# Moving a rarely taken branch and a residual addition inside a stream of expert products

## The chip, the core and the metric

The kernel runs on one core of a Trainium2 chip. That core has a matrix engine (TensorE, PE in the profile, with its weight loads as PEld), a vector engine (VectorE, DVE), a scalar engine (ScalarE, ACT), a general engine (GpSimd, POOL) and a queue engine (SyncE, SP) that here only starts transfers. Each engine runs its own list of instructions in order and waits for the others by semaphores. The metric is the device time of one execution in microseconds.

## The reference

Two layers of a decoder trunk on 256 tokens of width 1024. Each layer has a mixer (three groups of heads behind one projection, and an output projection), a layer norm, a mixture of experts, and a second layer norm. What the change touches is the mixture of experts and the addition before the second norm:

```python
for e in range(N_EXPERTS):                       # 16 experts, hidden width 512
    act = jax.nn.silu(t @ w_gate[e]) * (t @ w_up[e])
    out = out + combine[:, e:e + 1] * (act @ w_down[e])
...
h = layer_norm(DN_ALPHA * h + mix, ln_mix_g[layer], ln_mix_b[layer])
ffn = moe_ffn(h, router_w, router_bias, ...)     # top 2 of 16, within one group of 4
h = layer_norm(DN_ALPHA * h + ffn, ln_ffn_g[layer], ln_ffn_b[layer])
```

Each token goes to two experts; `combine` holds its two weights and zeros. All arithmetic is in float32.

## The kernel before

**Stages.** The mixer of a layer is put in order by a small planner (class `Order`, lines 75 to 236: it estimates when each engine comes free). The mixture of experts behind it (lines 1459 to 1622) is in the order in which its code is written, and the change lies there alone. That order is the same for both layers.

**Experts in pairs.** The loop of line 1538 runs over eight pairs of experts, `p` from 0 to 7. Instead of all 256 tokens, each expert works on 32 slots for each of the two tiles of 128 tokens (`CAP`, line 27): 128 rows for a pair. For each pair there are:
- a gather: one-hot matrices `G` (made on DVE) pick the tokens of two pairs at a time by products on PE, and ACT and DVE write them out scaled, as `xT` (`gather_two`, line 1326; after the up products of pairs 1, 3 and 5, `TWO`, line 59);
- 16 gate products, `gu`, then ACT's silu (line 1544), then 16 up products, in eight steps `k` of two (`step`, line 1514), then DVE's product of the two into `act` (line 1554);
- the pair's slot weights `Gw` (DVE, line 1351), turned on PE into a slot table `sT` and reduced by DVE (`by_slot`, line 1360);
- four transposes of `act` on PE, written out by ACT as `actT` (`turn`, line 1558);
- 16 down products `y` (line 1597), the loop index `i` of line 1593 counting eight steps of two;
- the weighting of their result by ACT and DVE into `yt` (`by_tile`, line 1379), and one pair later the scatter: four products `sc` of `yt` with the slot table, added to the sum `z` by DVE (`scatter`, line 1393).

**Weights.** Every expert matrix passes once through SBUF in tiles of 512 KB. SP issues them in the order of use; 33 buffers (`NFEED`) hold them, and a tile's transfer waits until the tile that had its buffer has been used (`used`, line 330, `more`, line 341). Some tiles are loaded ahead into other buffers (`EXTRA`).

**The overflow branch.** An expert can get more than 32 tokens of a tile. For that case `overflow()` (line 1407) holds a full calculation of all 16 experts on all tokens, with weights for the tokens left over, behind `tc.If(rmax > CAP)`: a compare-and-branch on every engine, on a count read into registers at the end of pair 0 (line 1622). With the inputs of this case it isn't taken. But PE's and DVE's programs hold its instructions, so both jump over them, and on the way past, each engine raises its own semaphore by what the instructions left out would have added. Six of the eight PSUM banks are handed out to it; whoever uses one of these banks next waits until the engines are past the branch. Where it stands is `OVER_AT`: behind up step 5 of pair 5.

**The residual.** `residual(t, n)` (line 1258) adds `alpha * (h * gain + bias)` to half `n` of tile `t` of the sum: three DVE operations `r`, `r`, `z` on 128 x 512. Gain and bias are vectors of the first norm, loaded by GpSimd and broadcast over the partitions (`lnvec`, line 372), in buffers that the down weights of pair 4 leave (`VECS`). `REST` names the four places: up steps 1 and 3 of pair 5 and up steps 1 and 5 of pair 6, as (pair, step).

Of the kernel before, what the change touches and what calls it, by code (L numbers as in the profile page):

```python
# [61 lines left out]
LEAN = 5  # L62
FILL_0 = (2, 3)
SC_AT = 5
OVER_AT = (5, 'u', 5)
REST = ((5, 1), (5, 3), (6, 1), (6, 5))
LAST_AT = 5
PARTED = (2, 3, 4, 5)
VECS = ((4, 2), (4, 3), (4, 5), (5, 3))
# [170 lines left out]
def trunk_kernel(ctx, tc, x, positions, w_in, gate_up, gate_bias, norm_gain, w_out, ln_mix_g, ln_mix_b,  # L240
# [18 lines left out]
    def t2(name, shape=(P, 512), dt=F32):  # L259
        return wp.tile(list(shape), dt, name=name, tag="t2", bufs=N_T2)  # L260
# [4 lines left out]
    def t1(name, shape, dt=F32):  # L265
        return wp.tile(list(shape), dt, name=name, tag="t1", bufs=N_T1)
# [63 lines left out]
    def used(l, p, nm, i, u):  # L330

        if type(u) is not list:
            more()
        elif (p, nm, i) in AGAIN:
            while specs[issued[0]][0] in extra:
                issued[0] += 1
            key, ((_, src),) = specs[issued[0]][0], specs[issued[0]][1][0]
            issued[0] += 1
            feed[key] = apart(place_of[p, nm, i], src)
# [150 lines left out]
    def mm(o, a, b, start=True, stop=True):  # L490
        pe.matmul(o, a, b, start=start, stop=stop, skip_group_check=True)
# [252 lines left out]
    for l in range(DEPTH):  # L744
# [513 lines left out]
        def residual(t, n):  # L1258

            c = slice(512 * n, 512 * n + 512)  # L1260
            r = t2("r")
            dve.scalar_tensor_tensor(r, h[t][:, c], ALPHA, vecs[0][:, c], op0=OP.mult, op1=OP.mult)
            dve.scalar_tensor_tensor(r, vecs[1][:, c], ALPHA, r, op0=OP.mult, op1=OP.add)
            dve.tensor_add(z[t][:, c], z[t][:, c], r)
# [86 lines left out]
        def weights(p):  # L1351

            Gw = t1("Gw", (P, NT, 2, NT * CAP))
            for t in range(NT):
                for e in range(2):
                    c = t * E + 2 * p + e
                    dve.tensor_scalar(Gw[:, t, e], iota, pos[:, c:c + 1], comb[:, c:c + 1], op0=OP.is_equal, op1=OP.mult)
            return Gw
# [20 lines left out]
        def by_tile(ps, ys, ws):  # L1379

            for y in ys:
                act.activation(y, ps, AF.Copy, scale=ws)
            for q in range(P // CAP):
                t = q % NT
                r = slice(q * CAP, (q + 1) * CAP)
                o = slice((q + 1 - 2 * t) * CAP, (q + 2 - 2 * t) * CAP)
                dve.scalar_tensor_tensor(ys[t][o], ps[r], ws[r], ys[t].bitcast(F32)[r], op0=OP.mult, op1=OP.subtract)
# [5 lines left out]
        def scatter(p, yt, sT, tiles=range(NT)):  # L1393
            if p == 0:
                z.extend(t4("z", (P, D)) for _ in range(NT))
            for t in tiles:
                for n in range(2):
                    b_ = bank("sc")
                    mm(b_, sT[:, t * P:(t + 1) * P], yt[n][t])
                    zs = z[t][:, 512 * n:512 * n + 512]  # L1400
                    if p == 0:
                        act.activation(zs, b_, AF.Copy)
                    else:
                        dve.tensor_add(zs, zs, b_)
                    od.free(b_)
# [87 lines left out]
        def part(u, j):  # L1493
            return u[j] if type(u) is list else u[:, j]
# [3 lines left out]
        def part_z(t, n):  # L1498

            if not zs:  # L1500
                zs["I"] = t1("identr", (P, P), F32R)
                act.activation(zs["I"], ident, AF.Copy)
            zs[t, n] = [t2("zs", dt=F32R) for _ in range(2)]
            split(z[t][:, 512 * n:512 * n + 512], *zs[t, n])
# [9 lines left out]
        def step(p, nm, b_, k):  # L1514
            if k % 2 == 0:
                us[nm] = [feed.pop((l, nm, p, k + e)) for e in range(2)]
            for e in range(2):
                mm(b_[64 * e:64 * e + 64], xs[p](k, e), part(us[nm][e], k % 2), start=k == 0, stop=k == KT - 1)
                if k % 2:
                    used(l, p, nm, k - 1 + e, us[nm][e])  # L1520
            if (p, nm) == (FIN, "u") and k in PARTED:
                part_z(*divmod(PARTED.index(k), 2))
            if (p, nm, k) == (FIN, "g", SC_AT):
                scatter(*late.pop())
            if (p, nm, k) == OVER_AT:
                overflow()
            if nm == "u" and (p, k) in REST:
                residual(*divmod(REST.index((p, k)), 2))

        def gate(p, upto):  # L1530

            if p not in gates:
                gates[p], done_k[p] = bank("gu"), 0
            while done_k[p] < upto:
                step(p, "g", gates[p], done_k[p])
                done_k[p] += 1

        for p in range(E // 2):
            final = p == FIN
            if final:  # L1540
                Gw = weights(p)
            gate(p, KT)
            av = t2("act")
            act.activation(av, gates[p], AF.Silu)
            if not final:
                Gw = weights(p)
            if p in TWO:
                G = t1("G", (P, NT, 4, CAP))
                for t in range(NT):
                    slots(G[:, t], t, 2 * p + 2)  # L1550
            bu = bank("gu")
            for k in range(KT):
                step(p, "u", bu, k)
            dve.tensor_mul(av, av, bu)
            od.free(gates[p], bu)
            sT, ws = by_slot(Gw, final)

            def turn():
                b_ = bank("aT")
                b3 = b_.rearrange("p (a n) -> p a n", a=4)  # L1560
                for f in range(4):
                    tr(b3[:, f], av[:, f * P:(f + 1) * P])
                aT = t2("actT", (P, 4, P))
                act.activation(aT, b3, AF.Copy)
                od.free(b_)
                made.append(aT)

            made = []
            if final:
                for n in range(2):  # L1570
                    for t in range(NT):
                        begin(t, n)
                turn()
            elif p == 0:
                gate(1, FILL_0[0])
                turn()
                gate(1, FILL_0[1])
            elif p in TWO:
                gather_two(p + 1, turn, G)
                scatter(*late.pop())  # L1580
            else:
                scatter(*late[0], (0,))
                if p < LEAN:
                    gate(p + 1, FILL[0])
                turn()
                scatter(*late.pop(), (1,))
                if p < LEAN:
                    gate(p + 1, FILL[1])
            aT, = made
            py = [bank("y") for _ in range(2)]  # L1590
            yt = [None, None]
            ud = [feed.pop((l, "d", p, i)) for i in range(8)]
            for i in range(8):
                n, k = (i // 4, i % 4) if p >= FIN - 1 else (i % 2, i // 2)
                for e in range(2):
                    u = ud[2 * k + e]
                    mm(py[n][64 * e:64 * e + 64], aT[:, k, 64 * e:64 * e + 64], part(u, n), start=k == 0, stop=k == 3)
                    if n:
                        if (p, 2 * k + e) in VECS:
                            vecs.append(lnvec((ln_mix_g, ln_mix_b, ln_ffn_g, ln_ffn_b)[len(vecs)], l))  # L1600
                        else:
                            used(l, p, "d", 2 * k + e, u)
                if k == 3:
                    yt[n] = [t2("yt", dt=F32R) for _ in range(2)]
                    if final:
                        split(py[n], *yt[n], scale=ws)
                    else:
                        by_tile(py[n], yt[n], ws)
                if final:
                    t = i - LAST_AT  # L1610
                    if t in range(NT):
                        place(sb[t, 0], t, 0, yt, sT, start=False)
                        sts.append(sm("st", 12).rearrange("p (a b) -> p a b", a=2))
                        dve.bn_stats(sts[t][:, 0], sb[t, 0])
            od.free(*py)
            late.append((p, yt, sT))
            if p == FIN - 1:
                more(2)
                if l + 1 < DEPTH:
                    mixer_constants(l + 1)  # L1620
            if p == 0:
                rmax = nc.values_load(cnti[0:1, 0:1], min_val=0, max_val=L)
# [68 lines left out]
```

## Time and profile before

| what | value |
|---|---|
| median of 3 runs | 736.85 us (736.49 to 737.7) |
| the profiled execution | 737.43 us, span 735.7 us |
| mean granted clock of PE | 0.987 |
| PE busy | 696.5 us, 95% |
| DVE busy | 441.1 us, 60% |
| ACT busy | 269.3 us, 37% |
| read from HBM | 241.08 MB, 329 GB/s over the span |

The span runs from the first to the last instruction in the profile. Times in the rows below are counted from its start. The expert stage of the first layer lies at about 160 to 355 us, that of the second at about 515 to 720 us. A share of busy time is a mean over stages with different limits; where PE waits is told by the list of waits and the timeline. The name behind an arrow in brackets is what ended the wait; `DVEq` and `PEq` are the sequencers of these engines, the parts that take branches and semaphores.

### The profile page before, as it was taken

The page shows a single profiled execution, that of the slowest core. Times are in us where ns is not written, and L with a number is a line of the kernel's source. Part 1 is how long each engine was busy: PE and PEld are TensorE (multiplying, and loading weights), DVE is VectorE, ACT ScalarE, POOL GpSimd, SP SyncE. Part 2 cuts the span into 40 slices and gives each one's busy share as a digit, 9 for nine tenths or more (in the row PEclk, how much of TensorE's full clock was granted, in tenths as well). Part 3 has the DMA queues.
Part 4 walks back from the last instruction along what each step waited for, and adds up shares of the span by engine and source line. Part 5 has one row for each costly group of instructions (what it writes and reads, how often), then busy time and mean ns, then how long its engine had stood idle before and what let it go on. Part 6 is the DMA issues. An engine that isn't in the chain of part 4 may idle for free. (4 is left out here: it accounts for less than half of the span.)

```text
span 735.7 us, 11107 instructions
## 1 busy us (share of the span) xinstructions
PE 696.5 (95%) x3817; PEld 403.2 (55%) x3817; DVE 441.1 (60%) x1115; ACT 269.3 (37%) x549; POOL 44.5 (6%) x72
## 2 busy tenths in 40 slices
PE   7999999999999997999899999999999999959993
PEld 6897977853533432533488788787334343334331
DVE  4897865652454546675498688566244263636645
ACT  5668645431211201212376766564113111102111
POOL 2000001000000001010130000001000000110002
PEclk9999999999999999999999999999999999989997
DMA  8899846879999999999999554667899999999921
GB/s 302 292 393 408 313 150 200 311 265 411 409 402 407 409 408 408 406 408 401 351 387 393 195 172 127 235 195 303 337 406 406 405 407 410 408 406 406 408 91 57
DMA packets 83245, 243.01 MB, mean 330 GB/s; under 512 B 10148, under 2 KB 14312, under 8 KB 83176
## 3 DMA queue, kind: packets, MB, share of 16 engines
q1 hardware_dynamic: 82504, 241.86, 86.5%
q8 instruction: 34, 0.56, 0.3%
q10 hardware_dynamic: 416, 0.26, 0.1%
q14 instruction: 35, 0.29, 0.1%
q0 software_dynamic: 256, 0.03, 0.0%
HBM read 241.08 MB, written 1.05 MB: 329 GB/s over the span
## 5 line engine op out<-in xcount | busy, mean ns | idle before, releaser
L235 PE MATMUL gu<-wf,xT 128*64 128x512 f32 x912 | 226.0, 594 | 3.8 <-PEq L1412 3.8
L235 DVE SCALAR_TENSOR_TENSOR yt<-y,ws,yt 32x512 fp32r<-32x512 f32 (+1 forms) x116 | 86.7, 747 | 103.3 <-ACT yt L235 101.8
L235 PEld LDWEIGHTS gu<-wf,xT 128*64 128x64 f32 x912 | 71.4, 137 | 132.3 <-issue 124.9
L235 DVE TENSOR_TENSOR wlo<-wf,whi 128x512 fp32r<-128x512 f32 (+2 forms) x174 | 97.3, 599 | 38.8 <-ACT whi L235 36.4
L235 PE MATMUL y<-wf,actT 128*64 128x512 f32 x432 | 110.5, 595 | 1.8 <-ACT actT L235 1.8
L235 ACT ACTIVATE whi<-wf 128x512 fp32r<-128x512 f32 (+2 forms) x176 | 86.8, 552 | 13.9 <-PE po L235 9.5
L235 PE MATMUL pj<-whi,hhi 128*128 128x512 f32 (+2 forms) x224 | 81.6, 364 | 0.0
L235 PE MATMUL pj<-wlo,hhi 128*128 128x512 f32 (+2 forms) x224 | 78.1, 349 | 1.7 <-DVE wlo L235 1.5
L235 PE MATMUL pj<-whi,hlo 128*128 128x512 f32 (+2 forms) x224 | 77.8, 347 | 0.0
L235 ACT ACTIVATE yt<-y,ws 128x512 fp32r<-128x512 f32 x60 | 36.9, 688 | 104.5 <-PE y L235 90.9
L235 PEld LDWEIGHTS y<-wf,actT 128*64 128x64 f32 x432 | 34.0, 137 | 54.1 <-issue 42.9
L235 DVE TENSOR_TENSOR act<-act,gu 128x512 f32<-128x512 f32 x16 | 11.0, 688 | 76.7 <-PE gu L235 52.4
L235 PE MATMUL gu<-wx,xT 128*64 128x512 f32 x112 | 52.7, 596 | 0.0
L235 PEld LDWEIGHTS pj<-whi,hhi 128*128 128x128 f32 x224 | 42.1, 188 | 8.3 <-issue 2.9
L235 PEld LDWEIGHTS pj<-wlo,hhi 128*128 128x128 f32 x224 | 42.1, 188 | 7.2 <-DVE wlo L235 3.5
L235 PEld LDWEIGHTS pj<-whi,hlo 128*128 128x128 f32 x224 | 42.1, 188 | 5.2
L235 ACT ACTIVATE xT<-xT,cols 128x256 f32<-128x256 f32 x32 | 17.4, 565 | 74.6 <-PE xT L235 74.6
L235 ACT ACTIVATE actT<-aT 128x512 f32<-128x512 f32 x16 | 9.5, 595 | 81.8 <-PE aT L235 81.8
L235 ACT ACTIVATE act<-gu 128x512 f32<-128x512 f32 x16 | 9.6, 597 | 75.7 <-PE gu L235 75.7
L235 PE MATMUL y<-wx,actT 128*64 128x512 f32 x80 | 33.4, 595 | 0.0
L235 DVE TENSOR_TENSOR z<-z,sc 128x512 f32<-128x512 f32 x48 | 29.7, 680 | 0.3 <-PE sc L235 0.2
L235 PE MATMUL xT<-G,z 128*128 128x128 f32 x128 | 19.7, 318 | 8.2 <-DVEq L1412 7.1
(269 smaller groups left out, 936.6 us busy)
## 6 DMA issues: line engine op xcount, KB each, us to landing
wf<-in_w_expert_gate_dram SPq DMA_DIRECT2D x114, 512.0 KB, 10.1
wf<-in_w_expert_up_dram SPq DMA_DIRECT2D x114, 512.0 KB, 10.1
wf<-in_w_expert_down_dram SPq DMA_DIRECT2D x108, 512.0 KB, 9.5
wf<-in_w_in_dram SPq DMA_DIRECT2D x32, 512.0 KB, 10.3
wx<-in_w_expert_down_dram SPq DMA_DIRECT2D x36, 256.0 KB, 6.6
wf<-in_w_out_dram SPq DMA_DIRECT2D x16, 512.0 KB, 10.5
wx<-in_w_expert_up_dram SPq DMA_DIRECT2D x24, 256.0 KB, 7.0
wx<-in_w_expert_gate_dram SPq DMA_DIRECT2D x10, 512.0 KB, 7.8
```

The costliest lines, as they stand in the source:

```text
L235: return fn(*a, **kw)
```

## The change

Two tables and two lines of code. The overflow branch goes from up step 5 of pair 5 to up step 0 of pair 4. The residual of tile 0 goes from the up steps 1 and 3 of pair 5 to the down steps 2 and 4 of the same pair, that of tile 1 from up steps 1 and 5 to up steps 0 and 2 of pair 6. For that, `REST` names the kind of product too, and the loop over the down products calls `residual`.

```diff
-OVER_AT = (5, 'u', 5)
-REST = ((5, 1), (5, 3), (6, 1), (6, 5))
+OVER_AT = (4, 'u', 0)
+REST = ((5, 'd', 2), (5, 'd', 4), (6, 'u', 0), (6, 'u', 2))
...
-            if nm == "u" and (p, k) in REST:
-                residual(*divmod(REST.index((p, k)), 2))
+            if (p, nm, k) in REST:
+                residual(*divmod(REST.index((p, nm, k)), 2))
...
+                if (p, "d", i) in REST:
+                    residual(*divmod(REST.index((p, "d", i)), 2))
```

DVE in the first layer, before, from the weighting of pair 4 (`yt`) to the product of pair 5 (`act`): the residual of tile 0 and then the branch stand ahead of that product. `avo` and `z<-ov` belong to the overflow code, whose other rows are left out.

```order
295 L235 SCALAR_TENSOR_TENSOR yt<-y,ws,yt 32x512 x8
296 L235 TENSOR_SCALAR Gw<-iota,pos,comb 128x64 x4
297 L235 TENSOR_TENSOR G<-iota,pos 128x128 x2
298 L235 SCALAR_TENSOR_TENSOR r<-h,vec 128x512
299 L235 SCALAR_TENSOR_TENSOR r<-vec,r 128x512
300 L235 TENSOR_TENSOR z<-z,r 128x512
301 L235 SCALAR_TENSOR_TENSOR r<-h,vec 128x512
302 L235 SCALAR_TENSOR_TENSOR r<-vec,r 128x512
303 L235 TENSOR_TENSOR z<-z,r 128x512
304 L1412 COMPARE_AND_BRANCH
...
337 L1412 UNCONDITIONAL_BRANCH x2
338 L235 TENSOR_TENSOR act<-act,gu 128x512
```

DVE in the same stretch now, from the slot weights of pair 5 to those of pair 6 (`yt` is pair 5's).

```order
330 L235 TENSOR_SCALAR Gw<-iota,pos,comb 128x64 x4
331 L235 TENSOR_TENSOR G<-iota,pos 128x128 x2
332 L235 TENSOR_TENSOR act<-act,gu 128x512
...
337 L235 TENSOR_SCALAR xT<-xT,cols 128x2x4x32 x4
338 L235 TENSOR_TENSOR z<-z,sc 128x512 x4
339 L235 SCALAR_TENSOR_TENSOR r<-h,vec 128x512
...
344 L235 TENSOR_TENSOR z<-z,r 128x512
345 L235 SCALAR_TENSOR_TENSOR yt<-y,ws,yt 32x512 x8
346 L235 TENSOR_SCALAR Gw<-iota,pos,comb 128x64 x4
```

The six residual operations have gone behind the scatter of pair 4 and ahead of the weighting of pair 5, and no branch is left between slot weights and product. The residual of tile 1 follows the slot weights of pair 6, as before.

DVE where the branch stands now: between the slot weights and the product of pair 4.

```order
287 L235 SCALAR_TENSOR_TENSOR yt<-y,ws,yt 32x512 x8
288 L235 TENSOR_SCALAR Gw<-iota,pos,comb 128x64 x4
289 L1412 COMPARE_AND_BRANCH
...
322 L1412 UNCONDITIONAL_BRANCH x2
323 L235 TENSOR_TENSOR act<-act,gu 128x512
```

PE where the branch stands now: behind 16 gate products and 2 up products of pair 4, with 14 up products behind it, then the slot transposes `sT` and the first scatter products `sc`.

```order
679 L235 MATMUL gu<-wf,xT 64x512 x18
680 L1412 COMPARE_AND_BRANCH
...
730 L1412 UNCONDITIONAL_BRANCH x2
731 L235 MATMUL gu<-wf,xT 64x512 x10
732 L235 MATMUL gu<-wx,xT 64x512
733 L235 MATMUL gu<-wf,xT 64x512
734 L235 MATMUL gu<-wx,xT 64x512
735 L235 MATMUL gu<-wf,xT 64x512
736 L235 MATMUL sT<-ident,Gw 128x128 x2
737 L235 MATMUL sc<-yt,sT 128x512 x2
```

Before, PE had 24 products ahead of the branch and 4 up products, the slot transposes and a gather behind it. SP, the difference of the two orders: the branch stands 26 weight transfers earlier.

```order
+L351 DMA wf<-in_w_expert_down_dram 128x1024 x2
+L1412 COMPARE_AND_BRANCH
+L1412 UNCONDITIONAL_BRANCH x2
+L351 DMA wf<-in_w_expert_down_dram 128x1024 x6
 L351 DMA wf<-in_w_expert_gate_dram 128x1024 x8
 L351 DMA wf<-in_w_expert_up_dram 128x1024 x8
-L351 DMA wf<-in_w_expert_down_dram 128x1024 x4
-L1412 COMPARE_AND_BRANCH
-L1412 UNCONDITIONAL_BRANCH x2
-L351 DMA wf<-in_w_expert_down_dram 128x1024 x4
+L351 DMA wf<-in_w_expert_down_dram 128x1024 x8
```

SP's transfers themselves keep their order. On GpSimd the branch goes from behind the third of four vector loads of a layer to ahead of the first.

## Rows read from the trace of the kernel before

**Rows 1.** The page: busy us and share, and transfers in 40 slices.

```profile
PE 696.5 (95%) x3817; PEld 403.2 (55%) x3817; DVE 441.1 (60%) x1115; ACT 269.3 (37%) x549; POOL 44.5 (6%) x72
...
DMA  8899846879999999999999554667899999999921
```

**Rows 2.** Waits of PE over the span: us in total, times, longest us.

```profile
PE xT L235 <- DVEq L1412: 9.4, 2, 7.1
...
PE gu L235 <- PEq L1412: 3.8, 2, 1.9
```

**Rows 3.** The branch's line: ns min/median/max, first and last start us.

```profile
L1412 PEldq COMPARE_BRANCH  x2: 6177/6179/6181, 283.8 to 641.7; - x2
...
L1412 DVEq COMPARE_BRANCH  x2: 63/68/72, 293.8 to 651.8; - x2
L1412 DVEq EVENT_SEMAPHORE  x2: 21/21/21, 294.5 to 657.4; - x2
L1412 POOLq COMPARE_BRANCH  x2: 50/52/53, 296.4 to 654.4; - x2
```

**Rows 4.** Timeline, first layer, pair 5: start us, us, instruction, [idle before <-releaser].

```profile
277.73 10.47 PE L235 MATMUL gu<-wf,xT 128*64 128x512 f32 x48
...
290.11 1.94 PE L235 MATMUL gu<-wf,xT 128*64 128x512 f32 x8 [1.91 <-PEq L1412]
...
291.03 0.69 DVE L235 SCALAR_TENSOR_TENSOR r<-vec,r 128x512 f32<-128x512 f32 x1 [4.46 <-POOL vec L376]
...
293.81 0.69 DVE L235 TENSOR_TENSOR z<-z,r 128x512 f32<-128x512 f32 x1
...
294.72 0.69 DVE L235 TENSOR_TENSOR act<-act,gu 128x512 f32<-128x512 f32 x1 [0.21 <-DVEq L1412]
```

**Rows 5.** Timeline of DVE, second layer, at the branch.

```profile
651.81 0.69 DVE L235 TENSOR_TENSOR z<-z,r 128x512 f32<-128x512 f32 x1
657.54 0.69 DVE L235 TENSOR_TENSOR act<-act,gu 128x512 f32<-128x512 f32 x1 [5.04 <-DVEq L1412]
```

**Rows 6.** Slot transposes to first down product: PE, PEld, DVE, ACT, POOL, clock, DMA.

```profile
291.98:300.00 8.02, 5.73 (x44) 5.08 (x42) 5.97 (x13) 2.75 (x5) 1.29 (x1) 1.00 1.03 405
649.96:664.87 14.91, 7.78 (x44) 7.12 (x43) 6.00 (x13) 2.86 (x5) 1.29 (x1) 0.77 1.03 405
240.82:246.32 5.50, 5.50 (x45) 5.05 (x43) 3.52 (x9) 2.75 (x5) 0.00 (x0) 1.00 1.03 407
598.80:604.30 5.50, 5.50 (x45) 5.05 (x43) 3.52 (x9) 2.75 (x5) 0.00 (x0) 1.00 1.03 409
```

**Rows 7.** Timeline of DVE, first layer, pair 4: slot weights and product.

```profile
260.02 0.98 DVE L235 TENSOR_SCALAR Gw<-iota,pos,comb 128x64 f32<-128x64 f32 x4
267.25 0.69 DVE L235 TENSOR_TENSOR act<-act,gu 128x512 f32<-128x512 f32 x1 [6.25 <-PE gu L235]
```

**Rows 8.** Timeline of DVE, first layer, down products of pair 5 and pair 6.

```profile
300.25 2.47 DVE L235 TENSOR_TENSOR z<-z,sc 128x512 f32<-128x512 f32 x4
307.65 6.08 DVE L235 SCALAR_TENSOR_TENSOR yt<-y,ws,yt 32x512 fp32r<-32x512 f32 x8 [4.94 <-ACT yt L235]
...
314.83 0.68 DVE L235 SCALAR_TENSOR_TENSOR r<-h,vec 128x512 f32<-128x512 f32 x1
...
320.97 0.69 DVE L235 TENSOR_TENSOR act<-act,gu 128x512 f32<-128x512 f32 x1 [1.95 <-PE gu L235]
```

**Rows 9.** Timeline of SP and PE, last down weights of both layers; issue to landing.

```profile
327.82 9.27 SPq L351 DMA_DIRECT2D wf<-in_w_expert_down_dram  x8
...
DMA to landing us min/median/max: 10.2/10.2/10.2
...
348.51 5.37 PE L235 MATMUL y<-wf,actT 128*64 128x512 f32 x24 [0.69 <-ACT actT L235]
...
685.67 9.80 SPq L351 DMA_DIRECT2D wf<-in_w_expert_down_dram  x8
...
713.38 5.37 PE L235 MATMUL y<-wf,actT 128*64 128x512 f32 x24 [0.69 <-ACT actT L235]
```

## The prediction

> **What bounds the kernel now.** Read first the page's busy shares and slices: TensorE (PE) is busy for 95% of the span, and the transfers run at nine tenths or more in every slice of the expert stages [rows 1]. So a microsecond counts only where PE waits or where it runs out of weights. Then the list of waits for PE alone: only two kinds name the branch, 9.4 us over two waits for VectorE's (DVE's) sequencer, the longer 7.1 us, and 3.8 us over two waits for PE's own sequencer [rows 2]. The other waits stand elsewhere in the program. Then the branch's own line: PE's compare-and-branch takes 6.18 us in either layer; DVE's is short, but DVE's first instruction behind it comes 0.7 us later in the first layer (293.8 to 294.5) and 5.6 us later in the second (651.8 to 657.4) [rows 3].
>
> The timeline of the first layer tells the order of events [rows 4]. PE's gate and up products of pair 5 run at 10.47 us for 48 half products, 0.436 us a product. The last two up steps start only at 290.11, after 1.91 us of idle time: PE's restart behind the branch, less what was already queued. DVE meanwhile stands in the residual: its second operation waits 4.46 us for the broadcast vector and starts at 291.03, the sixth ends at 294.50, and only then does DVE reach the branch; its product of gate and up starts at 294.72. PE's gather products need banks that the overflow code also holds, so they wait until DVE is past the branch. In the second layer the same wait is longer, because DVE is idle for 5.04 us after its last residual operation and before it is past the branch [rows 5].
>
> What this costs PE is read from one table. From the slot transposes of pair 5 to its first down product there are 8.02 us in the first layer and 14.91 us in the second; pair 3 does the same sequence (transposes, two halves of a gather, the turned activations, four scatter products) in 5.50 us in both, with PE busy in all of it [rows 6]. [...] Pair 3 is thus a measured price of pair 5 without branch and without residual ahead of it.
>
> **The change part by part.**
>
> Wait for DVE at pair 5: removed. No branch stands there any more, the banks of that gather were used again since the overflow held them, and DVE's order has its gate-times-up product directly behind the slot tables. Gain 8.02 - 5.50 = 2.52 us and 14.91 - 5.50 = 9.41 us [rows 6], 11.93 us together. From below: were only the two waits themselves gone, 9.4 us [rows 2]. The window value is taken, since it also holds the clock and the slower follow-up.
>
> PE's restart: moved. The branch now stands behind the first of eight up steps of pair 4, with 16 gate products and 2 up products ahead of it without a gap, as 24 products stood ahead of it before. So PE should show the same 1.91 us again in each layer. Bounds: 0, if the queue covers all of the 6.18 us, and 6.18, if it covers nothing [rows 3]: from -1.9 to +4.3 us a layer. I take 1.91, a change of zero, because the queue ahead is of the same kind.
>
> The wait at the new place: added. The first instruction that needs DVE past the branch is now the first scatter product of pair 4; behind it in PE's queue stand gate products of pair 5, the turned activations and all down products of pair 4. DVE reaches the branch behind the slot weights at 261.00 and had then been idle until its product at 267.25 [rows 7]: 6.25 us, and PE's own gap of 1.91 us makes it 8.2 us. The longest restart of DVE seen is 5.6 us. It fits with 2.6 us left; cost 0. If the cover went, PE would wait for the excess.
>
> ScalarE takes the branch behind the gate activation of pair 4 and has nothing to do until the turned activations, behind the same up products: 0. GpSimd now meets it ahead of all vector loads instead of between the third and the fourth, when it is idle until the down products of pair 4 release the first vector's buffer; its branch at 296.4 and 654.4 [rows 3] moves out of the row of loads: 0, or a little less. SyncE passes it 26 weight transfers earlier. Its queue holds several transfers of 512 KB in flight, 10.2 us from issue to landing [rows 9], so even 5.6 us for a restart would leave the transfers fed: 0.
>
> Residual of tile 0: moved to the down products of pair 5. DVE is idle there from 302.72 to 307.65, 4.93 us [rows 8]; six operations of 0.69 take 4.2 us. They fit with 0.7 us left, and the second vector, which the residual waited for until 291.03 [rows 4], has been there for 11 us. If they didn't fit, the weighting of pair 5 and what follows would move, and the next place where PE waits for DVE, the product at 320.97, has 1.95 us to give [rows 8]: 0. The residual of tile 1 stands between the same two operations of DVE as before, slot weights and product of pair 6; only its place in the source changes: 0.
>
> Weights, the new limit: the last eight down transfers of the first layer are issued from 327.82 over 9.27 us, so the last starts at 336.76 and lands, 10.2 us later, at about 347.0; its product, the eighth of pair 7, runs at about 351.5 [rows 9]. Lead 4.5 us, of which 2.52 are used. Second layer: last issue 695.1, landed at 705.3, needed at 716.4; lead 11.1 us. Of these 9.41 are used if the transfers of that layer come 2.52 us earlier together with PE, and 11.93 if they don't: 1.7 us left, or 0.8 us short.
>
> Sum: the profiled execution took 737.43 us (span 735.7). 737.43 - 11.93 = 725.50. It lay 0.58 above the median of the runs, so 724.9; I say 725.0.
>
> On the restart, DVE came back in 0.7 us in one layer and in 5.6 us in the other from the same code [rows 3]. [...] By the rows both fit the cover of 8.2 us, so the sum is the same.
>
> **The rivals.**
>
> The feed binds. For it: the transfers are at their ceiling [rows 1] and the lead falls to about 2 us in either layer. Against it: the landings computed above still come first. If the second layer's transfers don't move, PE loses 0.8 us; with a late SyncE restart eating 2 us in either layer besides, about 728.
>
> The queue covers the restart, and the two gaps of 1.9 us go: 725.0 - 3.8 = 721.2, but the lead of the first layer would then be 0.1 us and that of the second nothing, so the feed stops it at about 722.5. Against it: at the old place the queue held 6.18 - 1.91 = 4.27 us, about ten products, with the same kind of work ahead. [...]
>
> The whole restart shows at the new place, since PE's sequencer is held up just ahead of it: 6.18 instead of 1.91 in either layer, +8.5: 733.5.
>
> The wait follows the branch: DVE's restart takes longer than 8.2 us at the new place, and PE waits for the rest ahead of the scatter. At 11 us, twice what was seen, 2.8 us a layer: 730.6. That would mean that the branch is only displaced.
>
> Slower: PE's code. The restart brings one piece of code, and the next piece must be fetched the same way. At the old place PE waited for DVE right after the restart, which hid any second fetch. At the new place it has 14 products, 6.1 us, to run at once. If the first piece ends shortly behind the target and nothing is queued, PE pays a full 6.18 twice: 2 x 6.18 - 1.91 = 10.5 us a layer, 20.9 in all, against the gain of 11.93: 725.0 + 20.9 = 745.9. It turns the sign from 6.0 us of extra PE idle time a layer on.
>
> **How the numbers follow.** Forecast 72%, with its own range of 723.5 to 726.5; feed 9%; no gap 5%; whole restart 5%; wait follows 3%; a mixture of the last two that lands within 0.2% of before 2%; slower 4%. About 0.2%, 1.5 us, is what a measurement of this kernel can tell from no change. Faster: 72 + 9 + 5 + 5 + 3 = 94%. The range reaches down to the covered restart and up through the bound feed, 722 to 729.
>
> **What would show it.** Right: no PE wait that names the branch at the gather of pair 5, and 5.5 us from its transposes to the down products in both layers; a PE gap of 1.9 us behind the first up step of pair 4; DVE past the branch before PE's slot transposes of pair 4; six residual operations ending before the weighting of pair 5; a granted clock of 1.00 in that stretch of the second layer. Wrong: a PE wait for weights at the down products of pair 7, a wait for DVE's sequencer at the first scatter of pair 4, or two PE gaps behind the branch.

## The result and the profile after

| | before | after |
|---|---|---|
| median (runs of one sitting) | 737.28 us (736.49 to 737.73, 4 runs) | 724.08 us (723.63 to 724.72, 4 runs) |
| the profiled execution | 737.43 us, span 735.7 | 723.8 us, span 722.1 |
| mean granted clock of PE | 0.987 | 0.993 |

The ratio is 0.9823, 95% interval 0.9806 to 0.984. Forecast were 725.0 us and a range of 722 to 729; the change made the kernel 13.2 us faster, 1.3 us more than the sum had it.

First the page again, to set beside [rows 1]: busy us and share of each engine, and the transfers in 40 slices. PE's share rises by a point, and the transfers are as full as before, now farther into the last slices.

```profile
PE 692.0 (96%) x3817; PEld 400.0 (55%) x3817; DVE 440.7 (61%) x1115; ACT 269.1 (37%) x549; POOL 44.0 (6%) x72
...
DMA  9899845879999999999999755469799999999971
```

The list of PE's waits (us in total, times, longest) has lost its longest entry, the 9.4 us for DVE's sequencer of [rows 2]. The wait for PE's own sequencer is still there, and one small wait is new, the last of these rows.

```profile
PE gu L235 <- PEq L1412: 3.7, 2, 1.8
...
PE aT L235 <- DVE act L235: 0.4, 1, 0.4
```

The branch's line (ns min/median/max, first and last start) against [rows 3]: PE pays the same 6.1 us, now at 256 and 610 us. DVE reaches the branch at 258.9 and is past it at 264.5, in the second layer 613.1 and 618.7: 5.6 us in both layers, where before one layer had 0.7.

```profile
L1412 POOLq COMPARE_BRANCH  x2: 45/52/58, 158.7 to 512.8; - x2
...
L1412 PEldq COMPARE_BRANCH  x2: 6101/6109/6117, 256.3 to 610.5; - x2
L1412 DVEq COMPARE_BRANCH  x2: 68/70/72, 258.9 to 613.1; - x2
...
L1412 DVEq EVENT_SEMAPHORE  x2: 21/21/21, 264.5 to 618.7; - x2
```

The table of stretches, from the slot transposes of pair 5 to the first down product (us, then busy time and count of PE, PEld, DVE, ACT, POOL, clock, DMA, GB/s). These two rows answer to the first two of [rows 6], which were 8.02 and 14.91 us with a clock of 1.00 and 0.77:

```profile
291.53:297.04 5.51, 5.51 (x45) 5.05 (x43) 3.52 (x9) 2.79 (x5) 1.10 (x2) 1.00 1.02 406
645.72:651.23 5.51, 5.51 (x44) 5.05 (x43) 3.52 (x9) 2.79 (x5) 1.13 (x2) 1.00 1.03 409
```

PE is busy in all of both. Next the timeline of PE in the first layer, where the branch now stands (start, us, instruction, and in brackets the idle time before and what ended it). There is one gap of 1.85 us, and 20 matmuls run behind it without another; the second layer's row starts at 616.77 with a gap of 1.83.

```profile
252.84 7.89 PE L235 MATMUL gu<-wf,xT 128*64 128x512 f32 x36
262.58 4.51 PE L235 MATMUL gu<-wf,xT 128*64 128x512 f32 x20 [1.85 <-PEq L1412]
```

And the timeline of DVE in the same layer, at the branch and at the down products of pair 5, against [rows 7, 8]:

```profile
259.66 0.98 DVE L235 TENSOR_SCALAR Gw<-iota,pos,comb 128x64 f32<-128x64 f32 x4
268.92 0.69 DVE L235 TENSOR_TENSOR act<-act,gu 128x512 f32<-128x512 f32 x1 [8.28 <-PE gu L235]
...
299.66 0.68 DVE L235 SCALAR_TENSOR_TENSOR r<-h,vec 128x512 f32<-128x512 f32 x1
...
303.23 0.69 DVE L235 TENSOR_TENSOR z<-z,r 128x512 f32<-128x512 f32 x1
304.64 6.08 DVE L235 SCALAR_TENSOR_TENSOR yt<-y,ws,yt 32x512 fp32r<-32x512 f32 x8 [0.72 <-ACT yt L235]
```

At the branch DVE has 8.28 us between two operations, ended by PE and not by its own sequencer. Its sequencer had reached the branch at 258.9, while the engine still had the slot weights to do (they end at 259.66 + 0.98 = 260.64), and was past it at 264.5. That leaves 4.4 us to the product at 268.92, and 4.4 us in the second layer too (618.7 to 623.1). The six residual operations run without a wait in between and leave 0.72 us before the weighting.

**Where 13.6 us of span went.** Two stretches at pair 5: 8.02 - 5.51 = 2.51 and 14.91 - 5.51 = 9.40. A third was not in the sum: the gather of pair 0 in the second layer, far from the change. The same table for that stretch, of the kernel before and then of the changed one:

```profile
508.44:514.08 5.64, 5.64 (x36) 5.46 (x37) 2.25 (x12) 1.32 (x3) 0.00 (x0) 0.70 0.43 170
```

```profile
505.80:509.91 4.11, 4.11 (x36) 3.98 (x36) 2.24 (x12) 1.31 (x3) 0.00 (x0) 1.00 0.51 201
```

The same 36 matmuls with PE busy throughout, 1.53 us longer at a granted clock of 0.70: it was 0.50 from 508.40 to 511.80 and 1.00 from there to the end. In front of them PE has the same 1.08 us without work in both. With 0.3 us at the first loads, 0.1 us at the two gaps and the new 0.4 us of waiting the other way, 2.51 + 9.40 + 1.53 + 0.3 + 0.1 - 0.4 = 13.4 us of the 13.6.

### The profile page after: what moved, and what is told of

Read it like the earlier page. It is cut to its first block, busy times and chain, and to the rows that moved or that the text cites. A ratio compares the mean times of both kernels' runs of the same rounds, so it can differ in the third digit from the quotient of the medians.

```text
span 722.1 us, 11110 instructions
## 1 busy us (share of the span) xinstructions
PE 692.0 (96%) x3817; PEld 400.0 (55%) x3817; DVE 440.7 (61%) x1115; ACT 269.1 (37%) x549; POOL 44.0 (6%) x72
## 3 DMA queue, kind: packets, MB, share of 16 engines
HBM read 241.08 MB, written 1.05 MB: 335 GB/s over the span
## 5 line engine op out<-in xcount | busy, mean ns | idle before, releaser
L235 PE MATMUL sc<-yt,sT 128*128 128x512 f32 x72 | 23.8, 430 | 1.7 <-ACT yt L235 1.6
```

What stands on the lines that cost most here:

```text
L235: return fn(*a, **kw)
```

## The experiments

**1. The branch alone.** The branch at its new place, the residual at the old one.

```diff
-REST = ((5, 'd', 2), (5, 'd', 4), (6, 'u', 0), (6, 'u', 2))
+REST = ((5, 'u', 1), (5, 'u', 3), (6, 'u', 1), (6, 'u', 5))
```

> Only the branch is moved (behind up step 0 of pair 4); the residuals stay beside the up products of pairs 5 and 6. Theory (what PE lost at pair 5 was two things in a row on VectorE, the residual that waits for its vector, and then the branch): PE no longer waits ahead of the gather, but the product of pair 5 is still queued behind the residual, so the turned activations are late. In the first layer the vector is ready 1.7 us later than in the kernel before (its load starts behind the down products of pair 4, which the branch now delays), the product starts at about 296.3 instead of 291.7, and PE waits about 3.4 us ahead of the transposes of the activations, in both layers: 724.1 + 6.8 = 730.9 us. Rival 1 (the branch was the whole cost, the residual has cover): 724. Rival 2 (the residual was the whole cost): 737.

Measured 730.22 us (728.24 to 731.57), ratio 0.9913 (0.9889 to 0.9936). The list of waits, and PE's and DVE's timelines in the first layer:

```profile
PE aT L235 <- DVE act L235: 3.8, 3, 1.7
PE gu L235 <- PEq L1412: 3.6, 2, 1.9
```

```profile
291.80 0.69 DVE L235 SCALAR_TENSOR_TENSOR r<-vec,r 128x512 f32<-128x512 f32 x1 [3.12 <-POOL vec L376]
...
295.31 0.69 DVE L235 TENSOR_TENSOR act<-act,gu 128x512 f32<-128x512 f32 x1
```

```profile
296.05 0.65 PE L235 MATMUL aT<-ident,act 128*128 128x128 f32 x4 [1.69 <-DVE act L235]
```

Without any branch near it, the residual makes DVE's product late: it waits for the second vector until 291.80, its sixth operation ends at 295.28, and PE waits 1.69 us for the product (1.71 in the second layer). The expected 3.4 us a layer was twice too long; that the vector came 0.9 us sooner than thought is about half of the difference. That the median still lies near the expected 730.9 us is luck: the profiled execution (728.24 us) has 3.4 us of these waits in both layers together, and some 1.5 us of a lower-clock stretch in a gather (17.9 us of matmuls in the first layer's gathers, 16.4 in the second's), the effect of run 7 below; the two longest runs have a lower mean clock still (0.988 and 0.989, against 0.991). The kernel keeps about half of the gain: the residual costs PE time by itself.

**2. The residual alone**, the branch back at its old place, twice.

```diff
-OVER_AT = (4, 'u', 0)
+OVER_AT = (5, 'u', 5)
```

> Only the residuals are moved (the first two beside the down products of pair 5); the branch stays behind up step 5 of pair 5. Theory: VectorE now reaches the branch right behind the slot tables, at about 286.0 in the first layer, and even its longest restart, 5.6 us, ends at 291.6, before PE has done its last up products and slot transposes (292.0). PE's own gap of 1.9 us stands where it stood before. So no wait for VectorE is left and the time is that of the changed kernel, 724 us (723.5 to 725). Rival 1 (the earlier place of the branch gives the gain): about 731. Rival 2 (the residual has nothing to do with it): 737.

Measured 725.3 us (723.83 to 727.88), ratio 0.9851 (0.9826 to 0.9877). The branch's line for DVE:

```profile
L1412 DVEq COMPARE_BRANCH  x2: 63/68/72, 284.5 to 638.3; - x2
...
L1412 DVEq EVENT_SEMAPHORE  x2: 21/21/21, 285.9 to 643.8; - x2
```

DVE reaches the branch at 284.5 instead of 293.8, since no residual stands ahead of it, and is past it at 285.9 and 643.8, 1.4 and 5.5 us later. PE's slot transposes come only at about 292 and 646. The list of waits has no wait for DVE's sequencer. To compare with the whole change on one chip, both ran again side by side:

> The changed kernel itself, to compare on one chip. Expected 724.1 us, 723.5 to 725.5. Theory (the residual's move alone carries the gain): within 1 us of the kernel with only the residual moved. Rival (the branch's move adds something of its own): 1 us or more under it.

> Only the residual moved, branch at the old place behind up step 5 of pair 5, again, beside the changed kernel. Expected 724.5 us, 723.5 to 726. Theory: the restart of DVE is hidden at the old place too, once no residual stands ahead of it, so it agrees with the changed kernel within 1 us; what differs between single runs of either (723.8 at a mean granted clock of 0.994, 727.9 at 0.987 in the earlier run) is the clock. Rival (the old place has less cover, and DVE's restart shows in some executions): 1 us or more above the changed kernel, with a wait for DVE's sequencer in the list of PE's waits.

Measured: the changed kernel 724.15 us (723.49 to 726.36, ratio 0.9831, 0.9812 to 0.985), the residual alone 724.0 us (723.61 to 726.35, ratio 0.9827, 0.9808 to 0.9845). The medians agree within 0.2 us, and the runs at a clock of 0.993 or 0.994 lie within 1.1 us of each other, whichever of the two kernels it is. So the residual's move alone carries the gain, and the branch's move adds nothing to it that these runs can tell. It would have earned half of the gain without the other part, as run 1 shows; the two parts cure the same wait.

**3. No overflow code at all.** (`OVER_AT = None`; the kernel leaves out the overflow calculation.)

> The changed kernel without the overflow code and its branch (it leaves out the calculation for experts with more than 32 tokens of a tile, which these inputs don't need). Theory: PE's two gaps of 1.85 and 1.83 us go, 3.7 us, but the weights become the limit at the end of the second layer: the lead there is 1.05 us in the changed kernel, the transfers come 1.85 us earlier with the first layer and PE 3.7, so PE waits some 0.8 us for the last tiles: 724.1 - 3.7 + 0.8 = 721.2 us. Rival 1 (the feed doesn't bind): 720.4 with no wait for weights. Rival 2 (the gap is work that PE does anyway later): 724.

Measured 722.26 us (720.79 to 723.17), ratio 0.9799 (0.9775 to 0.9823). No entry of the branch is left in PE's waits, and none for weights has come. In the profiled execution the products behind the two former gaps come 1.9 and 2.0 us earlier against their neighbours ahead; some 1.5 us of that are lost to a lower-clock stretch at the gather of pair 0 in the second layer (17.9 us of matmuls in that layer's gathers, 16.4 in the first's). What the branch still costs the changed kernel is about 2 to 3 us. The expected wait for the weights did not come, but it was close: by their landings (an estimate from this trace) the last down tiles of pair 7 were there 0.1 and 0.6 us ahead of their products, the second with the help of the 1.5 us lost to the clock.

**4. The overflow code of one expert only**, so that the jump is short (the kernel leaves out the other 15 experts' overflow).

```diff
-                for e in range(E):
+                for e in range(1):
```

> The changed kernel with the branch in its place, but the overflow code holds one expert of 16 (it leaves out the other 15, which these inputs don't need), so that PE jumps over some 250 instructions instead of 3,400. Theory (PE's restart of 6.1 us is the fetch of code that is far away): the code behind the jump is at hand or on its way when PE gets there, the restart falls to well under 4.3 us and hides behind the queued products: no gap or one under 0.5 us, and a time near that without the branch, 721 to 722 us. Rival (every taken branch on PE costs its restart, whatever the distance, since the engine is emptied and started again): gap 1.8 us, 724 us.

Measured 721.64 us (720.58 to 722.5), ratio 0.9794 (0.9775 to 0.9813). The branch's line and the list of waits:

```profile
L1412 PEldq COMPARE_BRANCH  x2: 362/1014/1666, 256.8 to 609.0; - x2
```

```profile
PE gu L235 <- PEq L1412: 0.4, 2, 0.2
```

The same branch, at the same place, taken the same way: 0.36 and 1.67 us instead of 6.1. So the 6.1 us are not the price of a taken branch as such.

**5. The whole overflow as a loop.** The code is written once and looped over the 16 experts, `over` being shifted by one column at the end of each turn: 72 products stand behind the branch in PE's program instead of 912. By its code it would compute the same; like the code before it, it isn't taken with these inputs, so no run here shows that.

```diff
-                for e in range(E):
+                with tc.For_i(0, E, 1) as e:
...
+                    dve.tensor_copy(ovt[:, 0:2 * E - 1], over[:, 1:2 * E])
+                    dve.tensor_copy(over[:, 0:2 * E - 1], ovt[:, 0:2 * E - 1])
```

> The changed kernel, with the overflow code written as a loop over the 16 experts instead of 16 copies; the calculation that it would make is the same, and with these inputs it is not taken. The jump over it is then about as short as in the run that kept one expert's code. Theory (the restart is paid for the distance of the jump): no PE gap of 1.85 us behind the first up step of pair 4, at most 0.3 us in each layer; DVE past the branch in under 2 us; 721 to 722.5 us, that is 2 to 3.7 us under the changed kernel on the same chip; the lead of the last down weights falls to about 0.5 us but stays above zero. Rival (the restart is paid for a taken branch whose not-taken side holds more than one block of code, or for the registers of the loop): the gaps stay at 1.8 us and the time at 724 to 725.5 us.

Measured 722.44 us (720.9 to 723.88), ratio 0.9796 (0.9777 to 0.9815), 1.7 us under the changed kernel on the same chip. The branch's line, and PE behind it in the first layer:

```profile
L1413 PEldq COMPARE_BRANCH  x2: 328/345/362, 259.0 to 612.4; - x2
...
L1413 DVEq EVENT_SEMAPHORE  x2: 21/21/21, 263.4 to 616.7; - x2
```

```profile
263.63 1.04 PE L235 MATMUL gu<-wf,xT 128*64 128x512 f32 x3 [0.18 <-PEq L1413]
265.23 4.08 PE L235 MATMUL gu<-wf,xT 128*64 128x512 f32 x17 [0.56 <-issue]
```

PE's restart is 0.35 us and its gap 0.18, in the second layer 0.18 too. The 0.56 us in the second row are new: PE waits for nothing that the profile names, three matmuls behind the branch. Runs 7 and 8 come back to it. This profiled execution (723.88 us) had the lower clock in the gather of pair 0 in the first layer, 2.05 us for 8 matmuls that took 1.18 in the changed kernel and 5.04 for the next 24, there 3.07; the single runs of this kernel went from 723.88 us at a mean clock of 0.990 to 720.9 at 0.995.

**6. The loop at the old place**, with the residual at its old place too: the restart alone is taken away.

```diff
-OVER_AT = (4, 'u', 0)
-REST = ((5, 'd', 2), (5, 'd', 4), (6, 'u', 0), (6, 'u', 2))
+OVER_AT = (5, 'u', 5)
+REST = ((5, 'u', 1), (5, 'u', 3), (6, 'u', 1), (6, 'u', 5))
```

> Branch and residual at their old places, but the overflow code as a loop, so that the jump is short: the restart alone is taken away, the residual with its late vector stays ahead of DVE's product of pair 5. Theory (two causes, of which the late residual is the one that the first layer shows): PE's gap at the branch goes, but PE then waits that much longer for DVE's product in either layer, some 4 us from a first layer in which it was 2.4; the second layer becomes like the first, a gain of 14.91 - 8.02 = 6.9 us: 730.4 us, 729 to 732. Rival (the restart is the one cause, the residual is harmless): the whole 11.9 us and the two gaps of 1.9 us go, 721.5 us, 720.5 to 723.

Measured 730.67 us (728.07 to 733.01), ratio 0.9916 (0.9892 to 0.9941). The branch's line for DVE, PE's waits, and the stretch at pair 5 in both layers:

```profile
L1413 DVEq COMPARE_BRANCH  x2: 56/64/72, 293.0 to 648.3; - x2
L1413 DVEq EVENT_SEMAPHORE  x2: 21/21/21, 293.7 to 649.0; - x2
```

```profile
PE xT L235 <- DVEq L1413: 4.5, 2, 2.9
```

```profile
291.75:299.14 7.39, 5.73 (x43) 5.07 (x42) 5.80 (x12) 2.75 (x5) 1.29 (x1) 1.00 1.04 410
...
645.86:656.01 10.15, 7.29 (x44) 6.62 (x43) 7.17 (x14) 2.79 (x5) 1.29 (x1) 0.83 1.03 408
```

The time is the theory's, 730.4, and the rival's 721.5 falls: with a restart of 0.7 us for DVE in both layers, PE still waits at pair 5 in both, because DVE comes late out of the residual. The waits themselves were shorter than expected (1.66 and 2.87 us, expected some 4), so that the median falls on the expected time is in part the clock (0.987 to 0.989 in these runs). The second layer pays for its longer one again in clock: 10.15 us are 4.64 over the undisturbed 5.51, of which 2.87 are the wait and 7.29 - 5.51 = 1.78 the same matmuls at a clock of 0.83.

**7. Products on constants in PE's wait ahead of the gather of pair 0**, against the lower clock there; in the changed kernel, the kernel before and the loop.

```diff
                 slots(G[:, 0], 0, 0)
+                warm(3)
```

> The changed kernel with six products of 128 x 128 on constants more, between PE's product for the positions and the first product of pair 0's gather, in either layer: they fill 0.86 us of the 1.08 us in which PE waits there for DVE, and their results go nowhere. Theory (what the change gained over the 11.9 us of the sum, and what the single runs of one kernel differ by, is a stretch at the lower granted clock in that gather, which follows the wait): the mean granted clock is 0.993 or more in every run, all runs lie within 1 us of each other, median 723.5 us, and the gather of pair 0 takes 1.2 + 3.1 us in both layers. Rival (the lower clock falls there for another reason): the same spread as without them (723.5 to 726.4, clock 0.989 to 0.994), median 724.2.

> The kernel before with the same six products. Theory: about 1.5 us faster than the kernel before on the same chip, 735.5 us, clock up by some 0.002 to 0.003, so that the changed kernel with the six products is 12.0 us under it, the 11.9 us of the sum; the lower-clock stretch at pair 5 of the second layer stays. Rival: 737.1 us as without them, and the gain of the change 13 us again.

> The changed kernel with the overflow code as a loop and the same six products. Theory: runs at 0.994 or more, 720.5 to 721.8 us, median 721.0; three or so us under the changed kernel, with a lead of the last weights that stays above zero (0.5 us). Rival: 722.4 us with a spread of 3 us, as the loop had without them.

Measured: the changed kernel 727.15 us (727.02 to 728.07), ratio 0.9874 (0.9851 to 0.9898); the kernel before 737.0 us (735.87 to 737.95) beside 736.64 without them, ratio 1.0008 (0.9994 to 1.0022); the loop 721.94 us (721.12 to 722.35), ratio 0.9798 (0.9779 to 0.9818). Each of the three tells something else.

The clock did as expected in the changed kernel and in the loop: 0.994 in all runs of the first, 0.994 or 0.995 in those of the second, each within 1.3 us. The products took 1.58 us, not the 0.86 of the expectation, which had counted one matmul for each where the profile shows two, so they also cost some 0.2 us a layer (1.44 us from the start of the position's product to that of the gather, 1.25 without them). But the changed kernel lost 3.0 us, of which the products are 0.4. PE in its second layer, behind the branch:

```profile
617.85 3.62 PE L235 MATMUL gu<-wf,xT 128*64 128x512 f32 x15 [1.81 <-PEq L1413]
623.38 1.45 PE L235 MATMUL gu<-wf,xT 128*64 128x512 f32 x5 [1.92 <-issue]
```

A second gap of 1.92 us, 15 matmuls behind the first, most of what was lost: the second fetch of code, as the author reads it, which the prediction had among its rivals. The trace lists transfers of code under queues named `instruction`; for the two stretches 613 to 619 and 619 to 623 us of this kernel (packets, MB, share of 16 engines) `q8` shows one packet each:

```profile
q8 instruction: 1, 0.02, 1.1%
...
q8 instruction: 1, 0.02, 1.7%
```

The second packet landed at 621.96, and PE went on at 623.38. The changed kernel has the same two packets, in 612 to 618 and 618 to 622, without the second gap: there the second landed at 620.97, and PE ran its 20 matmuls from 616.77 on without a stop. The author's reading is that the first piece of code lasted until the second had come.

In the kernel before the theory failed. The products did remove the slow gather of the second layer, 1.5 us in the profile, but this execution had another stretch at the lower clock, behind PE's wait for DVE at pair 5 of the first layer:

```profile
295.30 2.63 PE L235 MATMUL xT<-G,h 128*128 128x128 f32 x16 [2.27 <-DVEq L1413]
297.72 1.06 PE L235 MATMUL aT<-ident,act 128*128 128x128 f32 x4
298.57 2.73 PE L235 MATMUL xT<-G,h 128*128 128x128 f32 x16
```

The kernel before had 2.12, 0.60 and 2.05 us there, behind a wait of 2.29 us. So the lower clock is not bound to the gather of pair 0. In the second layer of the kernel before, the granted clock was 0.50 at two of PE's waits: for 3.4 us behind the 1.08 us ahead of that gather, and from 655.2 to 662.0 us, in and behind the 7.1 us at pair 5. In the changed kernel's trace it was 1.00 behind the same 1.08 us. With the slow gather gone the time was where it had been, 737.0 beside 736.64 us, and the waits at pair 5 were still there; the change took these two waits away.

In the loop the restart of 6.1 us was back in one layer:

```profile
L1414 PEldq COMPARE_BRANCH  x2: 328/3230/6131, 256.8 to 610.8; - x2
```

```profile
263.06 4.51 PE L235 MATMUL gu<-wf,xT 128*64 128x512 f32 x20 [1.86 <-PEq L1414]
```

Twelve matmuls with their weight loads more, far ahead of the branch, and the same short jump costs 1.86 us of PE's time in the first layer and 0.19 in the second. All the same it is, with the loop without these products, the fastest kernel here that leaves nothing out: the two are alike against the kernel before of their own sittings (0.9798 and 0.9796), and with the products the runs lie closer together (1.2 us against 3.0).

**8. Fewer of these products in the changed kernel**, to test the second gap.

```diff
-                warm(3)
+                warm(2)
```

> The changed kernel with four products on constants in front of pair 0's gather instead of six (eight matmuls in the profile instead of twelve, 1.05 us instead of 1.58). With six, the second layer had a second PE gap behind the branch, 1.92 us, after 15 matmuls; the changed kernel itself has none there. Theory (the gap is a second fetch of code, and every matmul put ahead of the branch, with its weight load, moves the end of the code that the first fetch brought nearer to the branch's target): the second layer's target lies 8 matmuls farther from that end than with six products, at some 0.24 us each 1.9 us, so the gap shrinks to between 0 and 0.4 us; the clock stays at 0.993 or more, the runs lie within 1 us, and the median is 723.8 us, 723.2 to 724.8. Rival (the added products delay something else in the second layer, or the gap belongs to any change of the program there): a gap of about 1.9 us again, 726 us or more.

Measured 724.44 us (723.9 to 725.06), ratio 0.9831 (0.9817 to 0.9844). PE in the second layer, behind the branch, up to the place of the gap:

```profile
616.38 4.51 PE L235 MATMUL gu<-wf,xT 128*64 128x512 f32 x20 [1.83 <-PEq L1413]
...
621.13 0.59 PE L235 MATMUL gu<-wx,xT 128*64 128x512 f32 x1
621.82 0.59 PE L235 MATMUL gu<-wf,xT 128*64 128x512 f32 x1
```

There are 0.69 us from one start to the next where other pairs of rows have 0.40 or less: a gap of about 0.3 us is left, behind 23 matmuls instead of the 15 with six products. That is later by the 8 matmuls that the two layers have less ahead of it. The theory's numbers hold: 8 matmuls fewer ahead of the branch, and the gap came 8 matmuls later and fell from 1.92 to about 0.3 us. That it stands where a piece of code ends is the author's reading; no row shows that end. The clock was 0.993 to 0.995.

## Why the prediction was right, and where its size was off

**The wait at pair 5**: 11.93 us predicted, 2.51 + 9.40 = 11.91 measured. To take pair 3's stretch as the price of pair 5 without a wait was the right reading. The experiments say which part did it: the late residual, in both layers, with DVE's restart behind it in the second. The prediction credited branch and residual together and didn't see that either alone breaks the chain, wholly (the residual) or by half (the branch).

**PE's restart**: predicted 1.91 us again in each layer, measured 1.85 and 1.83. The queue ahead of the branch held 6.11 - 1.84 = 4.27 us, as much as before, so the rival without a gap and the one with the whole 6.18 fall. The price went with the code behind the branch: the same branch cost 6.1 us over 912 products and 0.33 to 1.67 us over a short stretch, and the short one cost 6.13 us in one layer when the code had shifted (runs 4, 5 and 7). DVE's restarts fall into two groups as well, 0.7 to 1.8 us and 5.5 to 5.7. Each of 5.5 or 5.6 us looked at here has one or two packets of 8 KB in the trace's other code queue, `q14`, while it lasts: one in the second layer of the kernel before, two in either layer of the changed kernel and in the second layer of run 2. Those of 0.7 us (kernel before, first layer) and 1.4 us (run 2, first layer) have none.

**The new wait at pair 4**: predicted hidden, with 8.2 us of cover, 5.6 of restart, 2.6 left. Measured were 8.28 of cover and 5.6 of restart, but 4.4 left: the prediction let DVE reach the branch only when the slot weights were done, and its sequencer was there 1.7 us earlier. DVE did pay the long restart in both layers, so the cover was needed.

**The residual beside the down products**: 0.7 us predicted to be left, 0.72 measured. The small wait of 0.4 us at pair 6 of the first layer was costed at zero. The kernel with the branch alone has it too (0.4 of its 3.8 us), and neither the kernel with the residual alone nor those of runs 3, 4 and 5, without a long jump, list it. So it goes with the long jump at the new place; by what way is not settled.

**Weights**: predicted a lead of about 2.0 us in the first layer and, in the second, of 1.7 us or 0.8 us too little. No wait for weights appeared. An estimate from the trace after, by the transfers' landings against the starts of their products, gives a least lead of 2.7 and 1.05 us for the down tiles of the last pair. The rival in which the feed binds falls, narrowly. (The transfers were not at nine tenths in every slice of the expert stages, as the prediction read [rows 1]: the second stage began at eight tenths and its last two slices had two and one.)

**Slower by a second fetch of code**: a second packet and a second gap of PE came in runs 7 and 8, the gap 15 and 23 matmuls behind the target, so the rival's condition (the first piece ends shortly behind the target) fits. Its price was too high: in the changed kernel's trace the second packet started at 619.90, 4.7 us after the first had landed and while PE's matmuls ran, and PE paid only what these left of some 5.5 us (3.62 of matmuls and 1.92 of gap in run 7; from 616.38 to 621.82, 5.44 us, in run 8). The changed kernel itself shows no second gap, which the author puts down to luck in how the code lay, on which the prediction had no row: with twelve more matmuls a layer the gap was there.

**The size.** The sum from the profiled execution gave 725.5 and that execution 723.8. The term that was missing is the clock away from the change: 1.53 us at the gather of pair 0 in the second layer, which the profiled execution of before ran at 0.70. The prediction took every stretch outside the change as fixed. Over several runs the gain was 13.2 and 12.9 us (737.28 - 724.08, 737.09 - 724.15), so it isn't one execution's chance alone; yet in run 7 the kernel before got nothing from curing this one place. That the kernel with fewer waits of PE had less of the lower clock is what the means show (0.987 before, 0.993 after); which wait gets it in a given execution stays open.

## What to carry to other kernels

When an in-order engine is late, look at everything that it has in its list ahead of the awaited instruction: the branch had the name in the list of waits, but the addition in front of it, waiting for a late vector, was what had to move. A rarely taken branch over much unrolled code cost PE 6.1 us in each layer here and DVE up to 5.7, with packets on the code queues meanwhile; written as a loop it cost PE 0.33 to 0.36 us in runs 5 to 7, but for one layer with 6.13, and either way it belongs where each engine has that much work queued or nothing to do. Sum up what a removed wait gives from an undisturbed copy of the same sequence, and add a margin for the clock away from the change, 1.53 us here.

## What the hardware showed that was not expected

- The price of one and the same jump was not fixed. The loop's branch cost PE 0.33 and 0.36 us in one program, and 0.33 and 6.13 us in another that had twelve more matmuls, with their weight loads, in each layer far ahead of it.
- The queue `q8` brought packets of 16 KB (34 in the page of either kernel), PE's code, as the times tell: PE went on 1.4 to 1.5 us after one had landed. So it was at the end of the long branch (landed 260.88 and 615.19 us in the changed kernel's trace, branch over at 262.41 and 616.60). It was the same at the gaps for which the profile names no wait: 1.92 us in run 7, about 0.3 in run 8, 0.56 in run 5 (landed 263.77, PE on at 265.23) and 0.39 in run 6 (289.00, 290.37).
- At the long jump a second packet followed 5.8 to 5.9 us after the first (started at 259.86 and 265.65, 614.10 and 619.90 us in the changed kernel's trace, at 287.30 and 293.20, 645.30 and 651.20 in that of the kernel before). The gaps of runs 7 and 8 are of this kind; those of runs 5 and 6 stand behind a short jump with one packet.
- The spread of single runs went with the mean granted clock. The changed kernel had 723.5 to 724.5 us at 0.993 or 0.994 and 726.36 at 0.989; with only the residual moved, 723.6 to 724.0 at 0.993 or 0.994, and 726.1 and 726.35 at 0.988 and 0.989. In the last of these the profile shows both gathers' matmuls slower, 17.9 us for the 128 of the first layer and 18.1 for those of the second, against 16.4 each in the changed kernel's. The second layer's rows:

```profile
L235 PE MATMUL xT<-G,z 128*128 128x128 f32 x128 | 18.1, 300 | 1.1 <-DVE top L235 1.1
```

```profile
L235 PE MATMUL xT<-G,z 128*128 128x128 f32 x128 | 16.4, 283 | 1.1 <-DVE top L235 1.1
```

(Groups of instructions by line: busy us, mean ns of one, and the idle time ahead of them with what ended it, 1.1 us in both.)
